# A gated block kernel on one Trainium2 core: values' hi and lo parts in one stationary operand, gate steps from output block 2, a lone step as one chunk

## The chip, the cores and the metric

The kernel runs on 1 core of one Trainium2 chip. The metric is the device time of one execution in microseconds (us). The kernel before takes 708.98 us, the median of 3 runs (708.42 to 709.07). The profile comes from one execution of 709.15 us, whose first and last instructions lie 707.1 us apart (the span).

## The reference

One residual block for 512 positions of 1024 features, one layer, batch 1, all in float32. Cut to what matters:

```python
proj = rms_norm(x, norm_mix_g) @ w_in
cb, cc, cin, q, k, v, f_logit, g_logit = split(proj)
y_conv = (cb * causal_dwconv(cc * cin, conv_mix_w)) @ w_out_conv
o = forgetting_attention(q, k, v, cumsum(log_sigmoid(f_logit + b_f)))   # 8 heads of 64
y_attn = o @ w_out_attn
g_conv, g_attn = split(sigmoid(g_logit + b_gate))                       # 1024 each
x = x + (g_conv * y_conv + g_attn * y_attn) @ w_o
a, b = split(causal_dwconv(rms_norm(x, norm_ffn_g) @ w_up, conv_ffn_w)) # 2816 each
x = x + (silu(a) * b) @ w_down
return rms_norm(x, norm_f_g)
```

## The kernel before, in words

**Products.** Everything is stored with features on the 128 partitions and the 512 positions along the free axis. Each float32 operand is kept as two parts, hi (its rounding to the matmul's input format) and lo (the rest). One product of a 128x128 weight block with activations is then three matmuls: hi weight with hi activation, lo weight with hi, hi weight with lo. `mm3` (L272, matmuls at L280) issues them for a whole block in two column halves of 256; `passes` (L286, matmuls at L298) does the same for a list of products.

**The stream of weights.** All weights come in chunks of up to 128x1024 in one fixed order, the list `stream` (L118 to L141). For a chunk, `load` (L157) starts the DMA on SyncE's queue into a raw tile (L170), several chunks ahead, and `split` (L230) makes the hi part on ScalarE (ACT, L249) and the lo part on VectorE (DVE, L253). These tiles are called raw_X, wh_X and wl_X after the chunk; wh and wl have two buffers each, so a split waits until TensorE is through with the chunk two ahead of it. Behind each split stands a budget in us by the chunk's kind, and `run_later` (L211) spends it: it takes work from the list `later`, whose items carry an assumed cost, and stops at the first one that is due and too dear. So `later` and those numbers fix where a small job stands in the in-order queues of ACT and DVE between two splits. `flush` issues what has to be done at once.

**Stages.** First the v projection, then those for q and k of two head pairs. Then the attention loop (L714 to L726): per unit (head pair, head, block of 128 queries) it issues the scores, half of another projection (`fill`) to keep TensorE busy, the transposes of the softmaxed scores of three units earlier (`transp`, tile tp; ACT writes their hi part pth, DVE at L605 their lo part ptl), and after each fourth unit `attend`. Scores use PSUM banks 3 and 4 in turn, transposes 5 and 6. During this loop DMA queues also make "forms", sums of weight blocks, in DRAM (`make_forms` L178: puts on SyncE's queue, accumulating DMAs on GpSimd's, one or two per loop slot).

`attend` (L607) forms, in bank 7 (tile o), the output of both heads of a pair for half of the queries. For each head e and block of keys it runs `mm3` with 128 columns of stationary weights, of which 64 are the head's values and 64 are zeros, so that both heads accumulate into the same 256 columns, each in its own 64 partitions. The values' hi and lo parts are two tiles, vh and vl. Then ACT copies o into oth (L621) and DVE subtracts into otl (L622).

**The merge stage** (L899 to L925) loops over eight output blocks j. For each it needs two gates: g(j) and g(8+j). For j = 0 to 2 they are plain projections (chunks in(20+j) and in(28+j), 48 matmuls each); the variable GJ = 3 says from which block on they come from `seven` (L743): a two-by-two block product in 7 instead of 8 products, with sums of weight blocks (the forms) and sums of activation blocks. Such a step of two products has a P chunk (18 matmuls) and an F chunk with the DMA-made forms (24 matmuls); an output block takes P, F, P, F. It writes four PSUM banks, (0, 1, 5, 6), where the products' sums are then combined (`gate_pair`). The activations' sums are made once from a fresh copy of x, xt: GpSimd's queue loads it (L809), ACT scales it by the norm's gain (L816, eight instructions), DVE forms sums (L824 to L829), ACT makes the hi part xth (L835) and DVE the lo part xtl (L836). This work is in `later` from chunk mix1 on. Then follows chunk mix(j), 48 matmuls into two banks, yc and ya; DVE multiplies them by the gates (L921, L922), GpSimd adds (L923), ACT and DVE split into mh and ml (L924, L925). The banks come from `acc`, a ring in the order 3, 4, 5, 6, 0, 1, 2, 7: mix0 has 3 and 4, in21 and in29 have 5 and 6, mix1 has 0 and 1, in22 and in30 have 2 and 7.

**The rest.** W_o, then the up projection and the gated unit in two phases, each followed by 7-product steps for W_down (20 steps of a P and an F chunk each; one step of phase 2 is a lone product, 9 + 12 matmuls), whose results `combine` adds to x1 (L1081 to L1099), also through `later`. For phase 2 it adds there `final_square` (L1107), per output block two ACT instructions and one DVE instruction into ssq, for the last norm. Two output blocks come from plain matmuls with the chunks dp0 to dp2 into banks 6 (pdA), 7 and 0 (pdB). The sums of squares go through pc_n and pb_n, and the output is scaled and written.

Of the kernel before, what the change touches and what calls it, by code (L numbers as in the profile page):

```python
# [50 lines left out]
)  # L51
HELD = 2

GJ = 3
GATES = tuple(((j, q), (j, q + 1)) for j in range(GJ, KB) for q in (0, 2))

PLAIN = [(m, k) for m in (6, 7) for k in range(*PHASES[1])]
# [7 lines left out]
def block_kernel(ctx, tc, xT, vecs, wv, win, wmix, wo, wup, wst, wdp, outT):  # L65
# [164 lines left out]
    def split(hl=None):  # L230

        k = len(parts)
        if k == len(stream):
            return
        nm, _, ncol = stream[k]
        load(k + (LOOK if len(raws) > KB else AHEAD))
        if hl is None:
            hl = []
            for x in "hl":
                if k == 0:  # L240
                    wp.tile([P, PADW[x]], F32, tag=f"pad{x}", name=f"pad_{x}")
                hl.append(wp.tile([P, D], F32R, tag=f"w{x}", name=f"w{x}_{nm}", bufs=2)[:, :ncol])
        hi, lo = hl
        raw = raws[k]
        if k == 0:
            for cs in (slice(0, VW), slice(VW, S + H)):
                keep(nc.vector.tensor_copy(hi[:, cs], raw[:, cs]))
        else:
            ins = nc.scalar.activation(hi, raw, AF.Copy)  # L249
            order["hi"] = ins.ins  # L250
            if k < KB:
                keep(ins)
        ins = nc.vector.tensor_sub(lo, raw, hi.bitcast(F32))  # L253
# [98 lines left out]
    def ct(name):  # L352
        return ap.tile([P, S], F32, tag="ct", name=name, bufs=NCT)
# [12 lines left out]
    )  # L366


    vh = ap.tile([P, NT, 4, 3, HD], F32R, tag="vh", name="vh")
    vl = ap.tile([P, NT, 4, 3, HD], F32R, tag="vl", name="vl")  # L370
    for t in (vh, vl):
        nc.gpsimd.memset(t.bitcast(F32)[:, :, :, 1, :], 0.0)
# [27 lines left out]
    def square_x(kb):  # L400
        if kb == 0:
            keep(nc.scalar.activation(ssq, xs[kb], AF.Square))
            return
        sq = ap.tile([P, S], F32, tag="pp", name=f"sq{kb}", bufs=NPP)
        keep(nc.scalar.activation(sq, xs[kb], AF.Square))
        keep(nc.vector.tensor_add(ssq, ssq, sq))

# [197 lines left out]
        nc.vector.tensor_sub(tl[:, : qb + 1, rs], src, th.bitcast(F32)[:, : qb + 1, rs])  # L605

    def attend(pr, half):  # L607
        o = bank(7, f"o{pr}{half}")
        nk = 2 * half + 2
        for e in range(2):  # L610
            th, tl = PT.pop((pr, e, half))
            for kb in range(nk):
                cs = slice(P, 2 * P) if kb == nk - 1 else slice(0, 2 * P)
                wh = vh[:, kb, pr, e : e + 2, :].rearrange("p a b -> p (a b)")
                wl = vl[:, kb, pr, e : e + 2, :].rearrange("p a b -> p (a b)")
                mm3(
                    o[:, cs], wh, wl, th[:, kb, cs], tl[:, kb, cs],
                    e == 0 and kb == 0, e == 1 and kb == nk - 1,
                )
        hs = slice(half * 2 * P, (half + 1) * 2 * P)  # L620
        nc.scalar.activation(oth[:, pr, hs], o[:, : 2 * P], AF.Copy)  # L621
        nc.vector.tensor_sub(otl[:, pr, hs], o[:, : 2 * P], oth.bitcast(F32)[:, pr, hs])  # L622


    def run_all(fs):
# [35 lines left out]
    def evac_v(g, t):  # L661
        p = (pa, pb)[g][t]
        src = p[:, : 4 * HD].rearrange("p (a b c) -> p a b c", a=2, b=2)
        pr = slice(2 * g, 2 * g + 2)
        for e in range(2):
            nc.scalar.activation(vh[:, t, pr, 2 * e, :], src[:, :, e, :], AF.Copy, scale=rc1[:, t : t + 1])
            nc.vector.scalar_tensor_tensor(
                vl[:, t, pr, 2 * e, :], src[:, :, e, :], rc1[:, t : t + 1],
                vh.bitcast(F32)[:, t, pr, 2 * e, :], op0=ALU.mult, op1=ALU.subtract,
            )  # L670


# [70 lines left out]
    def seven(doubles, n0, sets, operand, goes_on=None, stays=None, done=None):  # L743


        todo, wants = [], {}
        for n, d in enumerate(doubles):
            for kind in "PF":
                prods = []
                for s_, (i, q) in enumerate(d):  # L750
                    for f, g, b, h in PROD:
                        if (f < 3) == (kind == "P"):
                            wants.setdefault(f"{kind}{n0 + n}", []).append(("q", q))
                            c = 3 * s_ + f if f < 3 else s_ + len(d) * (f - 3)
                            prods.append((c, i, operand(q, g), b, h))
                todo.append((f"{kind}{n0 + n}", prods))
        users = [{(i, b) for _, i, _, b, _ in prods} for _, prods in todo]
        for n, (name, prods) in enumerate(todo):
            wh, wl = chunk(name)
            flush(wants[name])  # L760
            before = set().union(*users[:n])
            after = set().union(*users[n + 1 :])
            out = []
            for c, i, (xh, xl), b, h in prods:
                if i not in open_:
                    flush(sets[i])
# [7 lines left out]
            if name[0] == "F":  # L774
# [62 lines left out]

        return f

    k = [c[0] for c in stream].index("mix1")  # L840
    for q in (0, 2):
        f, g = x_sums(slice(q, q + 2))
        for i in (q, q + 1):
            later.append((k, 0, (("q", i),), x_scale(i)))
        later.append((k, 1.4, (("q", q),), f))
        later.append((k, 1.5, (("q", q),), g))
        for i in (q, q + 1):
            later.append((k + 1, 1.25, (("q", i),), x_split(i)))
        k += 2

    def gate_form(q, g):
        if g < 3:
# [219 lines left out]
    def combine(ph, i, banks, ids):  # L1072
# [248 lines left out]
```

## Time and profile before

| what | value |
|---|---|
| median of 3 runs | 708.98 us |
| the profiled execution | 709.15 us, span 707.1 us |
| TensorE (PE) busy | 99% of the span, 6054 matmuls |
| VectorE (DVE) busy | 70%, 766 instructions |
| ScalarE (ACT) busy | 48%, 525 instructions |
| GpSimd (POOL) busy | 25% |
| mean granted TensorE clock | 0.997 |

The profile gives times in us from the span's start; L12 is line 12 of the kernel. A group's row has its duration for one instruction in ns; the durations of matmuls overlap, so that their pitch has to be taken from starts. In a timeline the row begins with the start and the duration, and a bracket at its end gives the idle time of the engine before it and the instruction that ended it. The list of waits gives total, count and longest in us. A row of windows gives, for PE, weight loads, DVE, ACT and POOL, the busy us, then the granted clock, the DMA share and GB/s.

### The profile page before, as it was taken

The page shows a single profiled execution, that of the slowest core. Times are in us where ns is not written, and L with a number is a line of the kernel's source. Part 1 is how long each engine was busy: PE and PEld are TensorE (multiplying, and loading weights), DVE is VectorE, ACT ScalarE, POOL GpSimd, SP SyncE. Part 2 cuts the span into 40 slices and gives each one's busy share as a digit, 9 for nine tenths or more (in the row PEclk, how much of TensorE's full clock was granted, in tenths as well). Part 3 has the DMA queues.
Part 4 walks back from the last instruction along what each step waited for, and adds up shares of the span by engine and source line. Part 5 has one row for each costly group of instructions (what it writes and reads, how often), then busy time and mean ns, then how long its engine had stood idle before and what let it go on. Part 6 is the DMA issues. An engine that isn't in the chain of part 4 may idle for free. (4 is left out here: it accounts for less than half of the span.)

```text
span 707.1 us, 14653 instructions
## 1 busy us (share of the span) xinstructions
PE 696.6 (99%) x6054; PEld 694.6 (98%) x6054; DVE 494.6 (70%) x766; ACT 336.7 (48%) x525; POOL 174.0 (25%) x189
## 2 busy tenths in 40 slices
PE   9999999999999999999999999999999999999995
PEld 9999999999999999999999999999999999999995
DVE  6677767665477877854468777777774677877783
ACT  6664545453455544444354444445443345544562
POOL 5124847432101000134513223010000322311002
PEclk9999999999999999999999999999999999999998
DMA  7427979532451455687976856554636686676403
GB/s 249 165 73 246 198 201 205 111 89 68 129 208 53 149 183 175 198 281 188 222 177 170 211 118 147 141 178 159 203 128 227 142 194 154 179 188 165 145 26 119
DMA packets 52690, 116.02 MB, mean 164 GB/s; under 512 B 4976, under 2 KB 23408, under 8 KB 52624
## 3 DMA queue, kind: packets, MB, share of 16 engines
q1 hardware_dynamic: 37456, 94.16, 41.2%
q0 software_dynamic: 13760, 19.70, 17.5%
q10 hardware_dynamic: 1408, 1.24, 0.5%
q8 instruction: 47, 0.77, 0.5%
q14 instruction: 19, 0.16, 0.1%
HBM read 112.92 MB, written 33.03 MB: 206 GB/s over the span
## 5 line engine op out<-in xcount | busy, mean ns | idle before, releaser
L280 PE MATMUL p_up<-x1l,wh_up 128*128 128x256 f32 x536 | 104.5, 276 | 0.0
L280 PE MATMUL p_up<-x1h,wh_up 128*128 128x256 f32 x536 | 104.4, 276 | 0.0
L280 PE MATMUL p_up<-x1h,wl_up 128*128 128x256 f32 x536 | 104.3, 276 | 0.0
L249 ACT ACTIVATE wh_up<-raw_up 128x1024 fp32r<-128x1024 f32 x44 | 46.7, 1060 | 89.1 <-PE p_up L280 68.8
L280 PEld LDWEIGHTS p_up<-x1l,wh_up 128*128 128x128 f32 x536 | 80.8, 188 | 0.0
L280 PEld LDWEIGHTS p_up<-x1h,wh_up 128*128 128x128 f32 x536 | 80.7, 188 | 0.0
L280 PEld LDWEIGHTS p_up<-x1h,wl_up 128*128 128x128 f32 x536 | 80.6, 188 | 0.0
L253 DVE TENSOR_TENSOR wl_up<-raw_up,wh_up 128x1024 fp32r<-128x1024 f32 x44 | 53.8, 1223 | 20.6 <-ACT wh_up L249 20.6
L280 PE MATMUL p_in<-xgh,wh_in 128*128 128x256 f32 x288 | 56.9, 279 | 1.1 <-ACT wh_in L249 1.1
L1034 POOL TENSOR_TENSOR ge<-fu,fu 128x512 f32<-128x512 f32 x11 | 17.1, 1551 | 161.6 <-DVE fu L530 150.9
L280 PE MATMUL p_in<-xgl,wh_in 128*128 128x256 f32 x288 | 56.5, 277 | 0.0
L280 PE MATMUL p_in<-xgh,wl_in 128*128 128x256 f32 x288 | 56.4, 277 | 0.0
L198 POOL DMA_DIRECT2D f<-in_wst_dram x48 | 56.4, 1293 | 0.0
L1021 DVE TENSOR_TENSOR fz<-p_up,rb_n 128x512 f32<-128x512 f32 x44 | 30.3, 690 | 31.5 <-PE p_up L280 31.5
L253 DVE TENSOR_TENSOR wl_F<-raw_F,wh_F 128x1024 fp32r<-128x1024 f32 (+1 forms) x30 | 40.4, 1346 | 14.3 <-ACT wh_F L249 14.3
L280 PEld LDWEIGHTS p_in<-xgh,wh_in 128*128 128x128 f32 x288 | 44.7, 188 | 1.9 <-ACT wh_in L249 1.2
L249 ACT ACTIVATE wh_F<-raw_F 128x1024 fp32r<-128x1024 f32 (+1 forms) x30 | 31.6, 1052 | 30.3 <-PE dn L298 25.9
L280 PEld LDWEIGHTS p_in<-xgl,wh_in 128*128 128x128 f32 x288 | 43.6, 188 | 0.0
L280 PEld LDWEIGHTS p_in<-xgh,wl_in 128*128 128x128 f32 x288 | 43.5, 188 | 0.0
L298 PE MATMUL p_up<-x1h,wh_up 128*128 128x256 f32 x168 | 40.3, 277 | 0.0
L298 PE MATMUL p_up<-x1l,wh_up 128*128 128x256 f32 x168 | 40.2, 276 | 0.0
L253 DVE TENSOR_TENSOR wl_in<-raw_in,wh_in 128x1024 fp32r<-128x1024 f32 x26 | 34.7, 1336 | 7.3 <-ACT wh_in L249 6.8
(306 smaller groups left out, 2050.5 us busy)
## 6 DMA issues: line engine op xcount, KB each, us to landing
raw_up<-in_wup_dram SPq DMA_DIRECT2D x44, 512.0 KB, 4.7
raw_F<-f SPq DMA_DIRECT2D x29, 512.0 KB, 4.3
raw_in<-in_win_dram SPq DMA_DIRECT2D x26, 512.0 KB, 3.5
raw_P<-in_wst_dram SPq DMA_DIRECT2D x29, 384.0 KB, 3.9
f<-in_wst_dram POOLq DMA_DIRECT2D x29, 256.0 KB, 5.7
f<-in_wst_dram SPq DMA_DIRECT2D x14, 512.0 KB, 6.0
f<-in_wst_dram POOLq DMA_DIRECT2D x14, 512.0 KB, 8.1
f<-f SPq DMA_DIRECT2D x28, 256.0 KB, 4.6
```

The lines of the kernel that those rows point to most:

```text
L198: return lambda: keep(nc.gpsimd.dma_start(dst, src, accum_op=ALU.add))
L249: ins = nc.scalar.activation(hi, raw, AF.Copy)
L253: ins = nc.vector.tensor_sub(lo, raw, hi.bitcast(F32))
L280: keep(nc.tensor.matmul(out[:, cs], w, x[:, cs], start=start and i == 0 and c == 0, stop=stop and i == 2 and c == len(cut) - 1,))
L298: keep(nc.tensor.matmul(out, wl if x == 1 else wh, xl if x == 2 else xh, start=opens and bk not in seen, stop=closes and bk not in left,))
L1021: nc.vector.tensor_mul(z, p, rb2)
L1034: keep(nc.gpsimd.tensor_mul(ge, a.rearrange(halves_of, h=2), b.rearrange(halves_of, h=2)))
```

## The change

1. **Values.** vh and vl become one tile v2 that holds, for each head, the 64 columns of hi and the 64 of lo side by side. One matmul then gives hi and lo products at once, so that each head and block of keys takes two matmuls (with pth and with ptl) instead of three; it also adds the product of the two lo parts. The two heads go to separate halves of bank 7. The hi and lo products lie in different partitions, and so per head ACT copies one of them (L630) and DVE adds the other (L631) into a tile oc, before oth (L633) and otl (L634) are made from oc. The two memsets of the zero columns go.
2. **Gates.** GJ is 2: output block 2 takes P0, F0, P1, F1 (84 matmuls) instead of in22 and in30 (96). There are 12 gate steps instead of 10, and 6 groups of forms to be made by DMA instead of 5. The work on xt moves: it is due from chunk in29 on, with other assumed costs.
3. **Buffers.** One square tile of the first stage is allocated earlier, and the pool of xt waits for the last reader of each tile whose space it takes over.
4. **The lone step** is one chunk S (two DMAs, one split, 21 matmuls) instead of P and F.
5. **final_square** has the assumed cost 1.5 instead of 0.8 in `later`.

The core of the diff:

```diff
-GJ = 3
+GJ = 2
...
     def step_chunks(n):
         m = len(DOUBLES[n])
+        if m == 1:
+            return [(f"S{n}", n, NF * P)]
...
+            elif nm[0] == "S":
+                keep(nc.sync.dma_start(raw[:, : 3 * P], wst[src, :, : 3 * P]))
+                keep(nc.sync.dma_start(raw[:, 3 * P : ncol], made[src]))
...
-        run_later(k, {"u": 1.7, "P": 1.6, "F": 0.75, "i": 3.0, "m": 3.0}.get(nm[0], 3.5))
+        run_later(k, {"u": 1.7, "P": 1.6, "F": 0.75, "S": 1.6, "i": 3.0, "m": 3.0}.get(nm[0], 3.5))
...
+    v2 = ap.tile([P, NT, 4, 2, 2, HD], F32R, tag="v2", name="v2")
 
     ssq = ct("ssq1")
+    sq1 = ap.tile([P, S], F32, tag="pp", name="sq1", bufs=NPP)
...
     def attend(pr, half):
         o = bank(7, f"o{pr}{half}")
         nk = 2 * half + 2
         for e in range(2):
-            th, tl = PT.pop((pr, e, half))
+            parts_ = PT.pop((pr, e, half))
             for kb in range(nk):
-                cs = slice(P, 2 * P) if kb == nk - 1 else slice(0, 2 * P)
-                wh = vh[:, kb, pr, e : e + 2, :].rearrange("p a b -> p (a b)")
-                wl = vl[:, kb, pr, e : e + 2, :].rearrange("p a b -> p (a b)")
-                mm3(
-                    o[:, cs], wh, wl, th[:, kb, cs], tl[:, kb, cs],
-                    e == 0 and kb == 0, e == 1 and kb == nk - 1,
-                )
+                c0 = P if kb == nk - 1 else 0
+                w = v2[:, kb, pr, e, :, :].rearrange("p a b -> p (a b)")
+                for i, x in enumerate(parts_):
+                    keep(nc.tensor.matmul(
+                        o[:, 2 * P * e + c0 : 2 * P * (e + 1)], w, x[:, kb, c0:],
+                        start=e == 0 and kb == 0 and i == 0, stop=e == 1 and kb == nk - 1 and i == 1,
+                    ))
+        oc = ap.tile([P, 2 * P], F32, tag="oc", name=f"oc{pr}{half}")
+        for e in range(2):
+            own, other = slice(e * HD, (e + 1) * HD), slice((1 - e) * HD, (2 - e) * HD)
+            cs = slice(2 * P * e, 2 * P * (e + 1))
+            nc.scalar.activation(oc[own], o[other, cs], AF.Copy)
+            nc.vector.tensor_add(oc[own], o[own, cs], oc[own])
         hs = slice(half * 2 * P, (half + 1) * 2 * P)
-        nc.scalar.activation(oth[:, pr, hs], o[:, : 2 * P], AF.Copy)
-        nc.vector.tensor_sub(otl[:, pr, hs], o[:, : 2 * P], oth.bitcast(F32)[:, pr, hs])
+        nc.scalar.activation(oth[:, pr, hs], oc, AF.Copy)
+        nc.vector.tensor_sub(otl[:, pr, hs], oc, oth.bitcast(F32)[:, pr, hs])
...
-    xp = ctx.enter_context(tc.tile_pool(name="xp", bufs=1, side="right"))
+    xp = ctx.enter_context(tc.tile_pool(name="xp", bufs=1, side="right", reuse_waits="tile"))
...
-    k = [c[0] for c in stream].index("mix1")
-    for q in (0, 2):
-        f, g = x_sums(slice(q, q + 2))
+    k = [c[0] for c in stream].index(f"in{28 + GJ - 1}")
+    for q in range(4):
+        later.append((k, 0, (("q", q),), x_scale(q)))
+    for q, d, us in ((0, (0, 1), (1.4, 0.6)), (2, (1, 2), (0.9, 0.8))):
+        for f in x_sums(slice(q, q + 2)):
+            later.append((k + d[0], us[0], (("q", q),), f))
         for i in (q, q + 1):
-            later.append((k, 0, (("q", i),), x_scale(i)))
-        later.append((k, 1.4, (("q", q),), f))
-        later.append((k, 1.5, (("q", q),), g))
-        for i in (q, q + 1):
-            later.append((k + 1, 1.25, (("q", i),), x_split(i)))
-        k += 2
+            later.append((k + d[1], us[1], (("q", i),), x_split(i)))
...
-                later.append((0, 0.8, (), lambda m=m: final_square(m)))
+                later.append((0, 1.5, (), lambda m=m: final_square(m)))
```

The lines shift by 4 to 12: DVE's products L921 and L922 are L931 and L932 in the changed kernel, xt's sums L836 to L841, xtl L848.

**Where it moves instructions.** The first place is VectorE in the attention loop, around the attend of pair 2, second half (s and m are a unit's scores and row sums). Before:

```order
L577 ISA s312_2262,m312_2265<-s312_2262,strip_101 128x384
L577 ISA m312_2265 128x1
L622 TENSOR_TENSOR otl_95<-o21_2235,oth_94 128x256
L584 RECIPROCAL m312_2265<-m312_2265 128x1
L577 ISA s303_2313,m303_2316<-s303_2313,strip_101 128x512
```

In the changed kernel:

```order
L581 ISA s312_2260,m312_2263<-s312_2260,strip_101 128x384
L581 ISA m312_2263 128x1
L631 TENSOR_TENSOR oc21_2253<-o21_2236,oc21_2253 64x256
L588 RECIPROCAL m312_2263<-m312_2263 128x1
L631 TENSOR_TENSOR oc21_2253<-o21_2236,oc21_2253 64x256
L634 TENSOR_TENSOR otl_95<-oc21_2253,oth_94 128x256
L581 ISA s303_2311,m303_2314<-s303_2311,strip_101 128x512
L581 ISA m303_2314 128x1
```

Three instructions on oc and otl stand where one stood, each waiting for ACT's one ahead of it in the chain, and only a reciprocal stands between them.

The second place is the start of output block 2 in the merge stage. TensorE in the changed kernel, from the end of mix1 (ya1) into P0, with the rows that wait for another engine marked (dn025, dn020 and dn021 are the banks 5, 0 and 1):

```order
L285 MATMUL ya1_2802<-oth_94,wl_mix1_2725 128x256 x2
L285 MATMUL ya1_2802<-otl_95,wh_mix1_2724 128x256 x2
L303 MATMUL dn025_2858<-xgh_92,wh_P0_2790 128x256 [waits DVE_49,Activation_49]
L303 MATMUL dn025_2858<-xgl_93,wh_P0_2790 128x256
L303 MATMUL dn020_2856<-xgh_92,wh_P0_2790 128x256 [waits DVE_49]
L303 MATMUL dn020_2856<-xgl_93,wh_P0_2790 128x256
L303 MATMUL dn021_2857<-xth_2579,wh_P0_2790 128x256 [waits DVE_49]
L303 MATMUL dn021_2857<-xtl_2580,wh_P0_2790 128x256
```

Before, in22 stood there, with only its own weights to wait for:

```order
L280 MATMUL ya1_2792<-oth_94,wl_mix1_2713 128x256 x2
L280 MATMUL ya1_2792<-otl_95,wh_mix1_2712 128x256 x2
L280 MATMUL p_ga2_2846<-xgh_92,wh_in22_2780 128x256 [waits Activation_49]
L280 MATMUL p_ga2_2846<-xgh_92,wh_in22_2780 128x256
L280 MATMUL p_ga2_2846<-xgh_92,wl_in22_2781 128x256 [waits DVE_49]
L280 MATMUL p_ga2_2846<-xgh_92,wl_in22_2781 128x256
```

VectorE at the same place before (g1 and g9 are block 1's gates):

```order
L829 SCALAR_TENSOR_TENSOR xt_2582<-xt_2582 128x2x256
L253 TENSOR_TENSOR wl_in22_2781<-raw_in22_2545,wh_in22_2780 128x1024
L836 TENSOR_TENSOR xtl_2584<-xt_2582,xth_2583 128x1024 x2
L800 TENSOR_TENSOR g9_2788<-p_gb1_2727,rb_n1_530 128x512
L921 TENSOR_TENSOR g1_2724<-g1_2724,yc1_2791 128x512
L922 TENSOR_TENSOR g9_2788<-g9_2788,ya1_2792 128x512
L253 TENSOR_TENSOR wl_in30_2900<-raw_in30_2704,wh_in30_2899 128x1024
L925 TENSOR_TENSOR ml_2589<-g1_2724,mh_2588 128x512
```

and in the changed kernel:

```order
L258 TENSOR_TENSOR wl_P0_2791<-raw_P0_2544,wh_P0_2790 128x768
L840 SCALAR_TENSOR_TENSOR xt_2578<-xt_2578 128x2x256
L812 TENSOR_TENSOR g9_2798<-p_gb1_2739,rb_n1_527 128x512
L841 SCALAR_TENSOR_TENSOR xt_2578<-xt_2578 128x2x256
L931 TENSOR_TENSOR g1_2736<-g1_2736,yc1_2801 128x512
L848 TENSOR_TENSOR xtl_2580<-xt_2578,xth_2579 128x1024 x2
L932 TENSOR_TENSOR g9_2798<-g9_2798,ya1_2802 128x512
L258 TENSOR_TENSOR wl_F0_2879<-raw_F0_2700,wh_F0_2878 128x1024
L935 TENSOR_TENSOR ml_2585<-g1_2736,mh_2584 128x512
```

The product of g9 with ya1 came directly behind that of g1 with yc1, and has now two instructions on xtl ahead of it, as xt's work moved up to this place.

The third place is VectorE in the tail, around the split of dp0 (x1 is the residual, cz10 and cu10 belong to the combine of i = 0, cz11 to that of i = 1). Before:

```order
L1081 TENSOR_TENSOR cz10_8507<-dn2200_8264,cz10_8507 128x256
L253 TENSOR_TENSOR wl_P29_8535<-raw_P29_8344,wh_P29_8534 128x768
L1084 TENSOR_TENSOR x1_3968<-dn2206_8262,x1_3968 128x512
L1088 TENSOR_TENSOR cu10_8539<-dn2201_8265,cz10_8507 128x256
L1089 TENSOR_TENSOR x1_3968<-dn2207_8263,x1_3968 128x256
L253 TENSOR_TENSOR wl_F29_8561<-raw_F29_8374,wh_F29_8560 128x1024
L1092 TENSOR_TENSOR x1_3968<-x1_3968,dn2207_8263 128x512
L253 TENSOR_TENSOR wl_dp0_8590<-raw_dp0_8402,wh_dp0_8589 128x1024
L1095 TENSOR_TENSOR x1_3968<-x1_3968,cz10_8507 128x512
L1099 TENSOR_TENSOR x1_3968<-x1_3968,cu10_8539 128x512
L1084 TENSOR_TENSOR x1_3968<-dn2212_8441,x1_3968 128x512
L1115 TENSOR_TENSOR ssq3_4492<-ssq3_4492,sq3_0_8595 128x512
```

and in the changed kernel:

```order
L258 TENSOR_TENSOR wl_F31_8551<-raw_F31_8351,wh_F31_8550 128x1024
L258 TENSOR_TENSOR wl_dp0_8579<-raw_dp0_8407,wh_dp0_8578 128x1024
L1125 TENSOR_TENSOR ssq3_4498<-ssq3_4498,sq3_5_8582 128x512
L1091 TENSOR_TENSOR cz10_8586<-dn2400_8269,cz10_8586 128x256
L1094 TENSOR_TENSOR x1_3974<-dn2406_8267,x1_3974 128x512
L1098 TENSOR_TENSOR cu10_8590<-dn2401_8270,cz10_8586 128x256
L1099 TENSOR_TENSOR x1_3974<-dn2407_8268,x1_3974 128x256
L1102 TENSOR_TENSOR x1_3974<-x1_3974,dn2407_8268 128x512
L1105 TENSOR_TENSOR x1_3974<-x1_3974,cz10_8586 128x512
L1109 TENSOR_TENSOR x1_3974<-x1_3974,cu10_8590 128x512
L258 TENSOR_TENSOR wl_dp2_8600<-raw_dp2_8496,wh_dp2_8599 128x1024
L1125 TENSOR_TENSOR ssq3_4498<-ssq3_4498,sq3_0_8603 128x512
```

The combine of i = 0 (cz10 to its last x1) and a sum of squares moved from ahead of the split of dp0 to behind it.

More of the change, by code (lines that the diff above doesn't have):

```diff
@@ L366, in block_kernel @@
     )
[L369 to L372, printed above, removed]
+    v2 = ap.tile([P, NT, 4, 2, 2, HD], F32R, tag="v2", name="v2")
     ssq = ct("ssq1")
+    sq1 = ap.tile([P, S], F32, tag="pp", name="sq1", bufs=NPP)
     pa = [bank(t, f"pa{t}") for t in range(NT)]
@@ L403, in square_x @@
             return
-        sq = ap.tile([P, S], F32, tag="pp", name=f"sq{kb}", bufs=NPP)
+        sq = sq1 if kb == 1 else ap.tile([P, S], F32, tag="pp", name=f"sq{kb}", bufs=NPP)
         keep(nc.scalar.activation(sq, xs[kb], AF.Square))
@@ L665, in evac_v @@
         for e in range(2):
-            nc.scalar.activation(vh[:, t, pr, 2 * e, :], src[:, :, e, :], AF.Copy, scale=rc1[:, t : t + 1])
+            nc.scalar.activation(v2[:, t, pr, e, e, :], src[:, :, e, :], AF.Copy, scale=rc1[:, t : t + 1])
             nc.vector.scalar_tensor_tensor(
-                vl[:, t, pr, 2 * e, :], src[:, :, e, :], rc1[:, t : t + 1],
-                vh.bitcast(F32)[:, t, pr, 2 * e, :], op0=ALU.mult, op1=ALU.subtract,
+                v2[:, t, pr, e, 1 - e, :], src[:, :, e, :], rc1[:, t : t + 1],
+                v2.bitcast(F32)[:, t, pr, e, e, :], op0=ALU.mult, op1=ALU.subtract,
             )
@@ L747, in seven @@
         for n, d in enumerate(doubles):
-            for kind in "PF":
+            for kind in "PF" if len(d) > 1 else "S":
                 prods = []
@@ L751, in seven @@
                     for f, g, b, h in PROD:
-                        if (f < 3) == (kind == "P"):
+                        if kind == "S" or (f < 3) == (kind == "P"):
                             wants.setdefault(f"{kind}{n0 + n}", []).append(("q", q))
-                            c = 3 * s_ + f if f < 3 else s_ + len(d) * (f - 3)
+                            c = f if kind == "S" else 3 * s_ + f if f < 3 else s_ + len(d) * (f - 3)
                             prods.append((c, i, operand(q, g), b, h))
@@ L773, in seven @@
             passes(out, len(out))
-            if name[0] == "F":
+            if name[0] in "FS":
                 for i in sorted({i for _, i, *_ in prods}):
```

## The prediction

> **What bounds the kernel now.** I read the page's busy times and clock first, then TensorE's list of waits, then the timelines of the three places that the change touches.
>
> ```profile
> PE 696.6 (99%) x6054; PEld 694.6 (98%) x6054; DVE 494.6 (70%) x766; ACT 336.7 (48%) x525; POOL 174.0 (25%) x189
> ...
> PEclk9999999999999999999999999999999999999998
> ```
>
> TensorE is busy 696.6 of 707.1 us, at the full granted clock. What it waits for is short enough to list whole:
>
> ```profile
> PE p_in L280 <- ACT wh_in L249: 1.1, 1, 1.1
> PE warm L108 <- DVE ones L100: 1.0, 1, 1.0
> PE dn L298 <- ACT wh_F L249: 0.8, 1, 0.8
> PE pdA L280 <- DVE wl_dp L253: 0.3, 1, 0.3
> PE pc_n L313 <- ACT sq L1183: 0.3, 1, 0.3
> PE pb_n L327 <- POOL rc_n L320: 0.2, 1, 0.2
> ```
>
> They sum to 3.7 us. So a removed matmul is worth its full pitch, and other engines count only where they open a new hold of TensorE. There are two questions: how many matmuls go, and which holds appear.
>
> **The matmul's pitch.** The profile's 276 ns is a latency of overlapping matmuls. The pitch comes from starts:
>
> ```profile
> 97.55 0.37 PE L280 MATMUL o<-pth,vh 128*128 128x256 f32 x1
> ...
> 98.67 0.22 PE L280 MATMUL o<-pth,vh 128*128 128x128 f32 x1
> ...
> 98.95 0.33 PE L280 MATMUL o<-pth,vh 128*128 128x256 f32 x1
> ...
> 100.32 0.39 PE L572 MATMUL s<-a_k,a_q 128*128 128x384 f32 x1
> ```
> ```profile
> 188.89 0.45 PE L280 MATMUL yc<-ych,wh_mix 128*128 128x256 f32 x2
> ...
> 194.40 0.39 PE L280 MATMUL p_ga<-xgh,wh_in 128*128 128x256 f32 x2
> ```
> ```profile
> 205.28 0.39 PE L280 MATMUL yc<-ych,wh_mix 128*128 128x256 f32 x2
> ```
>
> The 96 matmuls of in21 and in29 lie between 194.40 and 205.28: 10.88/96 = 0.1133 us each. The second mix, 48 of them, takes 5.44. In attention the three 128-column matmuls from 98.67 to 98.95 take 0.28, 0.093 each.
>
> **Term 1, attention.** This view lists the tile o:
>
> ```profile
> L280 PE MATMUL o<-pth,vl x48: 273/276/283, 83.2 to 188.7; 128*128 128x256 f32 x32, 128*128 128x128 f32 x16
> ...
> L621 ACT ACTIVATE oth<-o x8: 378/384/385, 84.6 to 189.1; 128x256 fp32r<-128x256 f32 x8
> L622 DVE TENSOR_TENSOR otl<-o,oth x8: 415/420/422, 85.4 to 189.7; 128x256 fp32r<-128x256 f32 x8
> ```
>
> One such group of 48 goes (three products become two): 32 x 0.1133 + 16 x 0.093 = 5.1 us less. With 0.06 or 0.11 for a short one the bounds are 4.6 and 5.4. I take **-5.1**.
>
> In exchange each attend gets two ACT copies and two DVE adds, 16 of each, by the rows above 0.38 and 0.42 us and in a chain. They must stay hidden beside TensorE. DVE is fullest here:
>
> ```profile
> 120.00:130.00 10.00, 10.00 (x89) 10.00 (x88) 8.65 (x18) 6.28 (x15) 4.24 (x6) 1.00 0.56 146
> ```
> ```profile
> 125.27 0.27 PE L601 MATMUL tp<-ident,pp 128*128 128x128 f32 x1
> ```
> ```profile
> 121.49 0.68 DVE L605 TENSOR_TENSOR ptl<-tp,pth 128x512 fp32r<-128x512 f32 x1
> ```
>
> A transpose needs a PSUM bank that the ptl two units earlier has emptied: the one at 125.27 needs the ptl that ended at 122.17, 3.1 us of cover. In the changed order DVE waits inside the chain: from the first add to otl 3 x 0.42 + 2 x 0.38 = 2.03 us instead of 0.42, so later ptl come up to 1.6 late. That is under 3.1, so I cost it at 0; the other end is rival A. The sixth group of forms adds three POOL and three SP DMA issues; with POOL at 4.24 of 10 and the weights loaded far ahead I cost these at 0 too. The two memsets that go stand beside busy TensorE: 0.
>
> **Term 2, gate steps.** Block 2 takes 2 x (18 + 24) = 84 matmuls in steps instead of 96 in two projections: 12 x 0.1133 = **-1.4**.
>
> **Term 3, the hold at the first gate step.** Before, in22 stood behind mix1 and wrote banks 2 and 7. Now P0 does, and it writes banks 5, 0, 1; banks 0 and 1 are those of mix1's yc and ya. Its third matmul waits for DVE's g1*yc1 and its fifth for g9*ya1, which stands behind two xtl in DVE's queue (order rows above). The durations, all of before:
>
> ```profile
> 195.69 2.13 DVE L253 TENSOR_TENSOR wl_in<-raw_in,wh_in 128x1024 fp32r<-128x1024 f32 x1 [0.34 <-ACT wh_in L249]
> ...
> 203.02 0.69 DVE L824 TENSOR_TENSOR xt<-xt 128x512 f32<-128x512 f32 x1
> ...
> 206.63 1.23 DVE L253 TENSOR_TENSOR wl_in<-raw_in,wh_in 128x1024 fp32r<-128x1024 f32 x1 [0.67 <-ACT wh_in L249]
> 207.77 2.36 DVE L836 TENSOR_TENSOR xtl<-xt,xth 128x1024 fp32r<-128x1024 f32 x2
> 210.04 0.69 DVE L800 TENSOR_TENSOR g<-p_gb,rb_n 128x512 f32<-128x512 f32 x1
> 210.64 0.68 DVE L921 TENSOR_TENSOR g<-g,yc 128x512 f32<-128x512 f32 x1
> ```
> ```profile
> 194.60 1.06 ACT L249 ACTIVATE wh_in<-raw_in 128x1024 fp32r<-128x1024 f32 x1 [2.12 <-PE ya L280]
> 196.77 0.64 ACT L924 ACTIVATE mh<-g 128x512 fp32r<-128x512 f32 x1 [1.11 <-POOL g L923]
> ...
> 201.05 2.55 ACT L816 ACTIVATE xt<-xt,vec 128x512 f32<-128x512 f32 x4
> ...
> 206.50 1.99 ACT L835 ACTIVATE xth<-xt 128x1024 fp32r<-128x1024 f32 x2
> ```
>
> By starts a DVE instruction of 512 columns takes 0.60 in a row (210.04 to 210.64), a wl 1.14, the pair of xtl 2.27; on ACT an x scaling 0.62, an xth 1.0. Time 0 is mix0's start (188.89 before). wh_in29 starts at +5.7 before; now the sigmoids behind attend's longer chain end at +6.2, so it ends at +7.2. ACT then has all eight scalings (4.96), mh (0.55) and wh_mix1 (1.06): +13.8. DVE, which did wl_in29, four xt and ml meanwhile, goes on: wl_mix1 1.14, two xtl 2.27, then seven instructions (two xt, g1, xt's third and fourth, wl_P0 of 768 columns at 0.87, midway between 0.60 and 1.14, and g9), 6 x 0.60 + 0.87 = 4.5: +21.7. g1*yc1 ends at +22.3. The next xtl waits for its xth on ACT (1.05 after +21.7) and ends, with its twin, at +25.0; g9*ya1 ends at +25.75. TensorE: mix0, in21 with in29, mix1 are 5.44 + 10.88 + 5.44, so P0 starts at +21.76, its third matmul is due at +22.0 and held 0.3, its fifth is due at +22.5 and held 3.2. I take **+3.5**. Even directly behind ya's end (+22.0) the product would hold 0.5, the lower bound; were everything on DVE as slow as wl_in at 195.69 (2.13 for 1.23) it would be 5. F0's weights are due only at +27.9 and no second hold follows. xt itself is there: in before POOL issues it at 189.66 after this wait, now behind the last scores.
>
> ```profile
> 189.66 2.24 POOL L809 DMA_DIRECT2D xt<-in_xT_dram  x4 [12.87 <-PE o L280]
> ```
>
> **Term 4, the tail.** S29 has the 21 matmuls of P27 and F27. DVE's queue is the matter:
>
> ```profile
> 667.58 0.28 PE L298 MATMUL dn<-gh,wh_P 128*128 128x256 f32 x1
> ...
> 673.37 0.39 PE L298 MATMUL dn<-gh,wh_F 128*128 128x256 f32 x1 [0.83 <-ACT wh_F L249]
> ```
> ```profile
> 690.25 0.47 PE L313 MATMUL pc_n<-ones,ssq 128*128 128x1 f32 x3
> ```
> ```profile
> 679.01 1.23 DVE L253 TENSOR_TENSOR wl_dp<-raw_dp,wh_dp 128x1024 fp32r<-128x1024 f32 x1 [0.24 <-ACT wh_dp L249]
> ...
> 684.19 0.42 DVE L1081 TENSOR_TENSOR cz<-dn,cz 128x256 f32<-128x256 f32 x1
> 684.53 1.22 DVE L253 TENSOR_TENSOR wl_dp<-raw_dp,wh_dp 128x1024 fp32r<-128x1024 f32 x1
> ```
> ```profile
> 680.00:690.00 10.00, 9.71 (x85) 9.51 (x84) 9.64 (x18) 6.83 (x13) 0.00 (x0) 1.00 0.01 2
> ```
>
> From the lone step to pc_n it takes 690.25 - 667.58 = 22.67 now. The squares that ACT had ahead of wh_F go behind it: the 0.83 hold goes, and wl_dp0 comes at 11.43 - 0.83 = +10.6. But one ssq and five pieces of the combine of i=0, before ahead of wl_dp0, now stand behind it. From wl_dp0 to the last ssq DVE has 2 wl, 13 of 512 columns and 9 of 256 (0.34 by 684.19 to 684.53): 2 x 1.14 + 13 x 0.60 + 9 x 0.34 = 13.1, without a gap, since it was 9.64 of 10 busy already. pc_n at +23.8: **+1.1**. Bounds: -1.1 (both holds, 0.83 and 0.29, go and nothing is late) and +1.7 (ACT's last square adds a gap).
>
> **Sum.** -5.1 - 1.4 + 3.5 + 1.1 = -1.9 against the profiled execution's 709.15 (span 707.1 and 2.05 around it): 707.25. That execution lies 0.17 above the median of 708.98, so the forecast is **707.1**.
>
> **Rivals.**
> A, slower: attend's chain uncovers the transposes. Place: DVE between an attend and the next two ptl, where a 1.23 wl or 1.7 of other work follows. If half of the 1.6 us comes through at each of the eight, 6.4: **713.5**. From 0.24 per attend (1.9/8) the gain is gone. For it: 8.65 of 10 busy; against: 3.1 of cover.
> B: no long hold at P0, because DVE runs ahead or xtl is taken elsewhere: 0.5 instead of 3.5, **704.1**. Against it: DVE is in order, and xtl stands ahead.
> C: the hold lowers the clock.
>
> ```profile
> 700.00:708.00 8.00, 0.33 (x3) 0.14 (x2) 1.95 (x4) 0.39 (x1) 1.27 (x1) 0.66 0.38 131
> ```
>
> TensorE ended at 700.33, and a mean of 0.66 over 8 us, if the clock is 1 and then 0.5, means a fall at 702.6, 2.2 us later. A 3.2 us hold is longer. If matmuls then ran at half speed for as long as the hold, it costs 1.6 more: **708.7**. Against it: holds of 1.06 and 0.83 left the clock at 1.00. [...]
> D: the merged stationary operand gains nothing (128 columns of weights are loaded at each matmul and weight loads are 694.6 busy): only terms 2 to 4 are left, +3.2: **712.2**. Against it: pitch followed the count of matmuls in both places above.
>
> **How the numbers follow.** About 0.2% (1.4 us) is what a measurement can tell from no change. The forecast has 0.50, between 704.4 and 709.6 by its bounds: 0.32 of that faster, 0.18 same. A 0.14 (slower), B 0.18 (faster), C 0.12 (same), D 0.06 (slower). So faster 0.50, same 0.30, slower 0.20. The range takes in the forecast's, B and C and a mild A: 703.5 to 710.4.
>
> **What would show it.** Term 1: tile o with 96 matmuls, a second-half attend of 1.85 instead of 2.77, no tp among TensorE's waits (else A). Term 3: in the waits a dn held by DVE, 3 to 3.5 in all, with P0; near 0.5 means B, granted clock below 1 just behind it C. Term 4: no wh_F hold, pc_n held about 2 by ssq. If the time is over 710.4 without tp in the waits, D or a hold that I missed made the prediction wrong.

## The result, and the profile after

The changed kernel takes 709.93 us, the median of 12 runs (708.63 to 711.65), the kernel before 708.74 us (708.42 to 709.12, 12 runs): a ratio of 1.0013, with an interval of 1.0004 to 1.0022. It is a little slower, where 707.1 was forecast. The spread is part of the result: 3.0 us instead of 0.7. The runs lie on levels, and a level goes with the mean granted clock of the run:

| runs of the changed kernel | us | mean clock |
|---|---|---|
| 5 | 708.63 to 708.91 | 0.995 |
| 6 | 709.93 to 710.42 | 0.990 to 0.993 |
| 1 | 711.65 | 0.988 |

The kernel before has no such levels: its 41 runs beside the experiments lie between 708.3 and 709.3, with 0.995 to 0.998. The profiled execution took 708.69 us (span 706.5), so it is one of the lowest level. Even there the clock was not full throughout, as its windows below show.

First the page's busy times, then the top of TensorE's list of waits (total, times, longest, in us):

```profile
PE 691.2 (98%) x5994; PEld 689.1 (98%) x5994; DVE 503.5 (71%) x788; ACT 344.3 (49%) x543; POOL 175.1 (25%) x190
```
```profile
PE dn L303 <- DVE g L932: 3.0, 1, 3.0
PE pc_n L318 <- DVE ssq L1199: 2.1, 1, 2.1
PE p_in L285 <- ACT wh_in L254: 1.1, 1, 1.1
PE warm L108 <- DVE ones L100: 1.0, 1, 1.0
PE pdA L285 <- DVE x L1094: 0.6, 1, 0.6
...
```

The 60 matmuls that were to go are gone, and both holds stand where the prediction put them: P0 for g9*ya1, and pc_n for the last sum of squares. wh_F's hold of 0.8 is gone. No transpose waits.

TensorE's timeline at the places where the stages begin gives each term. The start of the first attend (the kernel before first, then the changed one), the second half of an attend, mix0, P0 with its hold, the lone step and pc_n:

```profile
82.98 0.37 PE L280 MATMUL o<-pth,vh 128*128 128x256 f32 x1
```
```profile
82.84 0.37 PE L622 MATMUL o<-pth,v 128*128 128x256 f32 x1
```
```profile
96.91 0.37 PE L622 MATMUL o<-pth,v 128*128 128x256 f32 x1
...
98.78 0.39 PE L576 MATMUL s<-a_k,a_q 128*128 128x384 f32 x1
```
```profile
183.32 0.45 PE L285 MATMUL yc<-ych,wh_mix 128*128 128x256 f32 x2
```
```profile
205.15 0.28 PE L303 MATMUL dn<-xgh,wh_P 128*128 128x256 f32 x1
...
205.82 0.28 PE L303 MATMUL dn<-xgl,wh_P 128*128 128x256 f32 x1
209.14 0.38 PE L303 MATMUL dn<-xth,wh_P 128*128 128x256 f32 x1 [3.04 <-DVE g L932]
...
210.90 0.28 PE L303 MATMUL dn<-xgh,wh_F 128*128 128x256 f32 x1
```
```profile
664.36 0.28 PE L303 MATMUL dn<-gh,wh_S 128*128 128x256 f32 x1
...
687.90 0.58 PE L318 MATMUL pc_n<-ones,ssq 128*128 128x1 f32 x4 [2.07 <-DVE ssq L1199]
```

An attend's second half takes 1.87 instead of 2.77 us, and mix0 starts 188.89 - 183.32 = 5.57 earlier. Of that, 0.14 lies ahead of the first attend; from there to mix0 it is 105.91 before and 100.48 now, 5.43 less. From P0 to F0 it is 5.75, where 18 matmuls take 2.04: 3.7 of hold and slower pitch around it. From the lone step to pc_n it is 23.54 instead of 22.67. At pc_n the changed kernel is 690.25 - 687.90 = 2.35 us ahead. At the end it is ahead by 0.6. The other 1.7 are lost behind pc_n, where no instruction changed. Windows of 3.41 us (the length for which the clock stays down in this trace; columns PE, weight loads, DVE, ACT, POOL, granted clock) show it:

```profile
682.12:685.54 3.42, 3.42 (x32) 3.42 (x32) 3.42 (x8) 1.01 (x2) 0.00 (x0) 1.00 0.00 0
685.54:688.95 3.41, 1.34 (x12) 1.18 (x11) 1.85 (x4) 2.86 (x7) 0.00 (x0) 0.99 0.00 0
688.95:692.36 3.41, 3.41 (x17) 3.41 (x18) 0.23 (x2) 0.00 (x0) 0.71 (x1) 0.51 0.02 5
```

Behind the hold of 2.1 the granted clock is 0.5 for 3.41 us, so half of that, 1.7 us, is lost; the count of matmuls in the window falls from 32 to 17.

### The profile page after: what moved, and what is told of

It is laid out like the page before. It is cut to its first block, busy times and chain, and to the rows that moved or that the text cites. A ratio compares the mean times of both kernels' runs of the same rounds, so it can differ in the third digit from the quotient of the medians.

```text
span 706.5 us, 14597 instructions
## 1 busy us (share of the span) xinstructions
PE 691.2 (98%) x5994; PEld 689.1 (98%) x5994; DVE 503.5 (71%) x788; ACT 344.3 (49%) x543; POOL 175.1 (25%) x190
## 4 chain that ended last, share of the span: by engine, by line
PE 92%; DVE 3%; ACT 3%; issue 1%; POOL 0%; DVEq 0%; ACTq 0%
PE p_up L285 26%; PE dn L303 21%; PE p_in L285 14%; PE p_up L303 8%; PE p_wo L285 6%; PE ya L285 2%; PE yc L285 2%; PE pa L439 2%; PE pb L441 2%; PE p_q L285 2%; PE p_k L285 2%; PE o L622 1%; PE tp L605 1%; PE pdB L285 1%; PE s L576 1%; PE s L577 1%
## 5 line engine op out<-in xcount | busy, mean ns | idle before, releaser
L203 POOL DMA_DIRECT2D f<-in_wst_dram x51 | 58.5, 1277 | 0.0
L258 DVE TENSOR_TENSOR wl_F<-raw_F,wh_F 128x1024 fp32r<-128x1024 f32 x31 | 42.1, 1359 | 14.4 <-ACT wh_F L254 14.4
L254 ACT ACTIVATE wh_F<-raw_F 128x1024 fp32r<-128x1024 f32 x31 | 33.0, 1066 | 26.9 <-PE dn L303 23.0
L254 ACT ACTIVATE wh_P<-raw_P 128x768 fp32r<-128x768 f32 x31 | 26.2, 844 | 29.6 <-PE dn L303 23.4
```

What stands on the lines that cost most here:

```text
L203: return lambda: keep(nc.gpsimd.dma_start(dst, src, accum_op=ALU.add))
```

## The experiments

Two theories stood against each other. Theory 1: the sum of the prediction holds at full clock, and each of the two holds also halves the clock for a while, which falls differently from run to run. The rival: holds cost their length and no more, and what is missing is a smaller gain elsewhere. All ratios are to the kernel before, run beside them.

**e1: part 1 alone.** The kernel before with the diff's v2, its filling and attend, nothing else.

> The kernel before with part 1 alone (values' hi and lo in one stationary operand). Theory 1 (the gain of attention is there in full, and what is lost is lost in two holds and in the clock behind them): mix0 starts 5.4 to 5.6 us earlier than before's 188.89, no tp in the list of waits, no hold over 1.1, granted clock as before (0.997) and a spread as narrow as before's 0.7: about 5.5 below the kernel before, 703.3. Rival (attend's longer chain holds the transposes, or merged operands gain less): less than 4 below it.

703.31 us (702.92 to 703.46, 4 runs), ratio 0.9921 (0.9908 to 0.9934). The profile's mix0 starts at 183.15, 5.74 earlier, of which 5.4 lies between the first attend and mix0 as in the whole change. The waits are those of the kernel before; its longest are:

```profile
PE warm L108 <- DVE ones L100: 1.0, 1, 1.0
PE p_in L280 <- ACT wh_in L249: 1.0, 1, 1.0
PE dn L298 <- ACT wh_F L249: 0.9, 1, 0.9
PE pdA L280 <- DVE wl_dp L253: 0.3, 1, 0.3
...
```

So attention's gain is there in full, and rival A (the transposes) is out. All that the whole change loses against this kernel, 6.6 us, comes from its other parts.

**e2 and e3: one hold taken away at a time.** In e2 mix1 has banks 2 and 7:

```diff
-    acc = ring(3, 4, 5, 6, 0, 1, 2, 7)
+    acc = ring(3, 4, 5, 6, 2, 7, 0, 1)
-                acc = ring(2, 7, 3, 4)
+                acc = ring(3, 4, 2, 7)
```

> The changed kernel with mix1 in banks 2 and 7 instead of 0 and 1, so that P0 waits for none of mix1's products. Theory 1: the hold of 3.3 at P0 goes; the tail's hold of 2.1 stays and halves the clock for one window of 3.4 us in some runs: two levels, 703.7 without and 705.4 with the drop, mean clock 0.997 and 0.995. Rival (the clock costs nothing, holds count by their length alone): one level, 709.9 - 3.3 = 706.6.

In e3 final_square has its old cost:

```diff
-                later.append((0, 1.5, (), lambda m=m: final_square(m)))
+                later.append((0, 0.8, (), lambda m=m: final_square(m)))
```

> The changed kernel with final_square's assumed cost back at 0.8. Theory 1: the tail's hold at pc_n goes (0.9 by the stage's length) and with it the clock's drop behind it (1.7); the hold at P0 stays and drops the clock in some runs: two levels, about 706.1 without and 707.8 with it. Rival (no cost by the clock): one level, 709.9 - 0.9 = 709.0.

| kernel | runs | us | mean clock |
|---|---|---|---|
| e2 (tail's hold left) | 4 | 704.82 to 705.29 | 0.997 |
| | 5 | 706.17 to 707.06 | 0.993 to 0.995 |
| | 3 | 708.11 to 708.43 | 0.991 |
| e3 (P0's hold left) | 1 | 705.40 | 0.997 |
| | 4 | 706.88 to 707.18 | 0.993 to 0.995 |

The levels are there in both, their means 1.4 to 1.9 apart, and the clock tells them apart; each hold drops it by itself. The medians are 706.24 (ratio 0.9965, 0.9954 to 0.9975) and 706.99 (0.9970, 0.9958 to 0.9982). The one-level rival is out. e3's two levels lie 0.7 to 0.8 below what was expected. e2 has a third level, and its undropped one lies 1.3 above what was expected. The list of waits says why: with P0's hold gone, F0 waits for wh_F, and block 2 from P0 to mix2 takes 10.94 instead of 84 x 0.1133 = 9.52.

```profile
PE pc_n L318 <- DVE ssq L1199: 2.1, 1, 2.1
...
PE dn L303 <- ACT wh_F L254: 0.7, 1, 0.7
PE pdA L285 <- DVE x L1094: 0.6, 1, 0.6
```

**e4: both edits.**

> The changed kernel with both edits: other banks for mix1 and final_square at 0.8. Theory 1: no hold over 1.1 is left, so the clock does not drop before the end: one level, 702.8 (708.7 - 1.7 - 3.3 - 0.9), spread under 1, mean clock 0.997. Rival (the clock costs nothing): 709.9 - 3.3 - 0.9 = 705.7; if another hold appears instead, its time is added.

703.27 us (702.85 to 703.52, 5 runs), ratio 0.9920 (0.9907 to 0.9933), mean clock 0.996 to 0.997: one level, as narrow as that of the kernel before, though 0.5 above the 702.8 expected. It is no better than part 1 alone (703.31), although block 2 has 12 matmuls less. In the profile P0 starts at 205.14, F0 at 208.04 and P1 at 211.32: 2.90 and 3.28 instead of 2.04 and 2.72. The hold moved to F0, whose wh stands behind two xth in ACT's queue:

```profile
208.04 0.38 PE L303 MATMUL dn<-xgh,wh_F 128*128 128x256 f32 x1 [0.70 <-ACT wh_F L254]
```
```profile
205.03 2.02 ACT L847 ACTIVATE xth<-xt 128x1024 fp32r<-128x1024 f32 x2
206.95 1.04 ACT L254 ACTIVATE wh_F<-raw_F 128x1024 fp32r<-128x1024 f32 x1
```

**e5 and e6: x's third and fourth split one chunk later**, with e4's banks and with those of the change:

```diff
-            later.append((k + d[1], us[1], (("q", i),), x_split(i)))
+            later.append((k + d[1] + (i >= 2), us[1], (("q", i),), x_split(i)))
```

> The kernel of e4 with x's third and fourth split (xth, xtl) one chunk later, behind F0's weights. In e4 the gate steps of block 2 won nothing: F0 waited 0.86 for wh_F and about 0.6 more up to P1, behind two xth and two xtl. Theory 1: these waits go: 703.3 - 1.5 = 701.8, one level. Rival (F0's weights are late by their DMA or by wh's buffer): 703.3 again.

> The changed kernel with final_square at 0.8 and x's third and fourth split one chunk later, banks as in the change. Theory 1: g9*ya1 stands directly behind g1*yc1, the hold at P0 is 0.5 to 0.7 and drops no clock: one level, 702.4. Rival (the bank itself, not the two xtl, makes the hold): 3 us of hold stay, 705.4 to 707.0 as in e3.

e5: 702.98 us (702.72 to 703.30, 5 runs), ratio 0.9918 (0.9904 to 0.9931). e6: 703.22 (702.99 to 703.41, 4 runs), 0.9920 (0.9906 to 0.9933). e6 shows that the two xtl made the hold at P0, not the banks by themselves: with them behind g9*ya1 the hold is gone while the banks are those of the change. But neither e6's 702.4 nor e5's 701.8 came. In e5 F0 starts on time, 2.04 behind P0, and P1 now takes 3.41 instead of 2.04, since it waits for the xtl that was moved:

```profile
210.66 0.28 PE L303 MATMUL dn<-xth,wh_P 128*128 128x256 f32 x1
212.01 0.39 PE L303 MATMUL dn<-xtl,wh_P 128*128 128x256 f32 x1 [1.07 <-DVE xtl L848]
```

**e7 and e8: the hold at P0 made shorter and longer**, both with final_square at 0.8. Theories 1a and 1b are two guesses of the author at how much of a window has to be idle, for these runs to decide between. In e7 only x's fourth split comes later (`(i == 3)` in the line above); in e8 the second xtl is computed three times over, with the same values:

```diff
-            nc.vector.tensor_sub(xql[:, q], xq[:, q], xqh.bitcast(F32)[:, q])
+            for _ in range(3 if q == 1 else 1):
+                nc.vector.tensor_sub(xql[:, q], xq[:, q], xqh.bitcast(F32)[:, q])
```

> The kernel of e3 with only x's fourth split one chunk later: one xtl less ahead of g9*ya1, a hold of 2.1 to 2.2 at P0. Without a drop of the clock 705.4 - 1.1 = 704.3. Theory 1a (a window of 3.4 us halves the next one if about two thirds of it or more are idle; 2.2 us are at most 64%): seldom or never a drop, 704.3 in all runs. Theory 1b (half of a window is enough): a drop in most runs, 705.9. [...]

> The kernel of e3 with the second xtl computed three times (the same values), 2.3 us more of VectorE ahead of mix1's products: a hold of about 5.5 at P0. Theories 1a and 1b: the clock drops in every run, for one window of 3.4 us or two: 705.4 + 2.3 + 1.6 = 709.3, or 711. [...] Rival (no cost by the clock): 707.7 in all.

e7: 706.22 us (5 runs): one of 704.38 and four of 706.19 to 706.53, ratio 0.9958 (0.9946 to 0.9971); its hold was 1.9. e8: 708.64 (708.01 to 709.81, 11 runs), ratio 0.9998 (0.9989 to 1.0006), mean clock 0.991 to 0.995 in every run; its hold was 4.4, not 5.5, so that by e3's 705.40 with 3.0 of hold it would stand at 706.8 at full clock, and every run lies 1.2 to 3.0 above that. So the clock costs something in every run of e8, as theories 1a and 1b had it. Theory 1a fell by e7: a hold of 1.9 was enough in four of five runs. The windows of the profiled executions say how much idling it takes. The three of e7 around P0, then two of the changed kernel at its P0 (no drop follows), then three of e8:

```profile
205.94:209.36 3.42, 1.46 (x10) 1.18 (x10) 2.83 (x4) 2.52 (x3) 0.86 (x1) 1.00 0.00 0
209.36:212.77 3.41, 3.41 (x18) 3.41 (x17) 3.41 (x4) 1.36 (x2) 1.33 (x1) 0.50 0.52 173
212.77:216.19 3.42, 3.42 (x32) 3.42 (x31) 1.70 (x2) 1.17 (x2) 0.00 (x0) 1.00 0.26 103
```
```profile
204.25:207.67 3.42, 1.79 (x14) 1.39 (x12) 2.83 (x5) 3.29 (x4) 0.00 (x0) 1.00 0.00 0
207.67:211.08 3.41, 1.94 (x16) 1.94 (x17) 2.55 (x3) 0.32 (x1) 1.91 (x1) 1.00 0.02 5
```
```profile
204.52:207.93 3.41, 1.51 (x12) 1.15 (x10) 3.41 (x6) 2.49 (x3) 0.00 (x0) 1.00 0.00 0
207.93:211.35 3.42, 0.95 (x3) 0.86 (x4) 3.42 (x5) 1.74 (x3) 0.33 (x1) 0.50 0.00 0
211.35:214.76 3.41, 3.41 (x17) 3.41 (x17) 1.54 (x3) 1.37 (x2) 1.86 (x1) 0.50 0.47 123
```

Of these windows, those with TensorE busy for 1.34 (the tail), 1.46 or 1.51 of 3.41 us were followed by half clock, those with 1.79 or 1.94 were not. That fits theory 1b. Behind e8's second window, busy for 0.95, the clock was at 0.50 in the third too. In the changed kernel's profiled execution, by an estimate from its fall at 688.89 (141 steps of 3.413 us back), a window's edge near 207.6 cut the long hold at P0 into two halves, and nothing followed: 1.00 up to 211.08.

But half of a window busy is not the rule, as the ends of the same kernels show. In e6 a window there is busy for 2.22 us and half clock follows; many of its matmuls are only one column wide (pc_n):

```profile
691.17:694.59 3.42, 2.22 (x15) 1.75 (x14) 0.38 (x2) 1.19 (x3) 0.87 (x2) 1.00 0.27 95
694.59:698.00 3.41, 0.00 (x0) 0.00 (x0) 1.73 (x4) 0.00 (x0) 1.10 (x1) 0.50 0.63 219
```
```profile
691.52 0.61 PE L318 MATMUL pc_n<-ones,sq 128*128 128x1 f32 x4 [0.27 <-ACT sq L1193]
691.99 0.96 PE L1216 MATMUL warm_to<-gl,gh 128*128 128x256 f32 x6
693.15 0.71 PE L332 MATMUL pb_n<-ident,rc_n 128*128 128x128 f32 x4 [0.20 <-POOL rc_n L325]
```

In e2 the 3.41 us ahead of a fall at 699.6 at the end (0.90 over the second row is 0.4 us at half clock) were busy for about 2.56:

```profile
696.00:698.00 2.00, 1.73 (x16) 1.64 (x15) 0.55 (x2) 0.92 (x2) 0.22 (x1) 1.00 0.54 190
698.00:700.00 2.00, 1.03 (x7) 0.64 (x5) 0.25 (x1) 0.38 (x1) 0.68 (x2) 0.90 0.00 0
700.00:706.00 6.00, 0.00 (x0) 0.00 (x0) 1.70 (x4) 0.00 (x0) 1.06 (x1) 0.50 0.50 175
```

What sorts the windows better is how many columns the matmuls begun in them move, counted in the timelines of the same profiles:

| clock in the window | columns, and where the window starts | clock in the next |
|---|---|---|
| 1.00 | 520 (changed kernel, 685.5), 2052 (e6, 691.17), 2304 (e7, 205.94, and e8, 204.52), 2560 (e2, 682.55) | 0.50 |
| 1.00 | 3072, 4096 and 3336 (changed kernel, 204.2, 207.6 and 695.7) | 1.00 |
| 0.50 | 768 (e8, 207.93), 2056 (e2, 685.96) | 0.50 |
| 0.50 | 3584 (e2, 689.38), 3840 (changed kernel, 688.9), 4096 (e7, 209.36) | 1.00 |

At the pitch of 0.1133, 30 matmuls of 256 columns, 7680, fit in a window. In the two profiles of the kernel before and the changed one, counted in steps of 3.413 us from their falls, no window at full clock with fewer than 3072, from 8 us on, was followed by full clock. One end does not fit, by an estimate: e5's last 2300 or so columns begin at 690.4 and are through at 693.60, but its mean clock of 0.998 over 700.5 us leaves about 2.8 us of half clock, a fall near 697.7, where e6 has it at 694.59 behind the like.

In two profiles the edges of the clock lie whole windows apart: in the changed kernel it falls at 688.89, rises at 692.30 and falls at 702.54, which is 1 and then 3 times 3.413 us; in e2 it falls at 685.96, rises at 692.79 and falls at 699.6, which is 2 and then 2 times. That the windows run on like this through an execution, that a hold falls on them differently from run to run and that the levels come from this is the author's estimate; no run shows an edge moved on purpose.

**e9: GpSimd scales xt**, behind its load, and x's third split goes back ahead of F0:

```diff
-                nc.scalar.activation(xt[:, kb, :], xt[:, kb, :], AF.Copy, scale=col(G1 + kb))
+                nc.gpsimd.tensor_scalar(
+                    xt[:, kb, :], xt[:, kb, :], col(G1 + kb), 0.0, op0=ALU.mult, op1=ALU.add
+                )
...
-        later.append((k, 0, (("q", q),), x_scale(q)))
+        x_scale(q)()
```

> The kernel of e5 with xt's scaling on GpSimd (eight instructions right behind its load) instead of ScalarE, and x's third split back ahead of F0's weights. In e5 the hold of block 2's first step only moved on, to P1's wait of 1.4 for xtl. Theory 1 (the work on xt is what limits the start of block 2, and ACT's eight scalings are its first 5 us): the chain comes some 1.4 us sooner and P1 waits no more: 703.0 - 1.4 = 701.6. Rival (wh_F0, which waits for the end of mix1 on TensorE, and not xt, sets when xtl can come; or GpSimd beside VectorE slows both): 703 or more.

703.15 us (702.55 to 703.26, 5 runs), ratio 0.9919 (0.9906 to 0.9933): nothing won, and theory 1 of this run fell. GpSimd had scaled xt by 183, but VectorE's first sum still ran only at 192.74, in its place in the queue. From wl_mix at 195.58 to the end of block 2's second wl_P VectorE has a single gap, of 0.55, and P1 waits for this wl_P:

```profile
211.02 0.94 DVE L258 TENSOR_TENSOR wl_P<-raw_P,wh_P 128x768 fp32r<-128x768 f32 x1
```
```profile
212.01 0.51 PE L303 MATMUL dn<-xgh,wl_P 128*128 128x256 f32 x2 [0.87 <-DVE wl_P L258]
```

So in e4, e5 and e9 three different instructions held block 2, for 1.5, 1.4 and 1.2 us in all. That points to VectorE's load in these 16 us, which none of the three lowers, as the cause behind them; sums ahead of mix0's products, where VectorE still has gaps, weren't tried.

In these 16 us an instruction of VectorE takes longer while GpSimd's addition of mix1's products runs. First e5's rows, then e9's:

```profile
206.11 2.10 DVE L258 TENSOR_TENSOR wl_F<-raw_F,wh_F 128x1024 fp32r<-128x1024 f32 x1 [0.35 <-ACT wh_F L254]
```
```profile
205.84 1.30 POOL L933 TENSOR_TENSOR g<-g,g 128x512 f32<-128x512 f32 x1 [14.44 <-DVE g L932]
```
```profile
208.17 2.32 DVE L850 TENSOR_TENSOR xtl<-xt,xth 128x1024 fp32r<-128x1024 f32 x1
```
```profile
207.20 2.21 POOL L935 TENSOR_TENSOR g<-g,g 128x512 f32<-128x512 f32 x1 [15.47 <-DVE g L934]
```

VectorE's instruction takes 2.1 to 2.3 there and 1.2 where nothing runs on GpSimd (1.21 for e5's xtl at 210.75 and e9's wl_F at 211.89). In e9 the wl_F under which the addition begins, at 207.03, takes 1.22, and the addition 2.21 instead of e5's 1.30. The 0.9 to 1.1 us more are about what P1 waits for in these two kernels. That the addition makes the wait is not shown: no run moves it away.

**e10: part 4 undone in e5**, that is, without the chunk S.

> The kernel of e5 with part 4 undone: the lone step is a P and an F chunk again. Theory 1 (part 4 matters only where ACT and DVE hold the tail): wh_F's hold of 0.8 comes back and pdA's of 1.2 goes to 0.3 as in the kernel before, between 702.9 and 703.6. Rival (the chunk S itself is a gain): 703.7 or more.

703.85 us (703.38 to 704.14, 5 runs), ratio 0.9928 (0.9916 to 0.9941). It is 0.9 above e5, with wh_F's hold of 0.9 back and pdA's of 1.2 down to 0.3. By the time alone the rival (703.7 or more) took it. The profiled executions lie 1.2 apart: 0.56 of that lies between the first down step of phase 1 and pc_n (212.18 against 211.62), and another 0.7 ahead of mix0 (183.63 against 182.94), where the two kernels do the same. So the chunk S is worth some 0.6 here, the most that theory 1 gave it, and theory 1's claim that it matters only where ACT and DVE hold the tail stays unproven.

## Why the prediction was wrong

Its sum was right for an execution at full clock, as far as that can be worked out; no run of the changed kernel had full clock throughout. The profiled execution fell short of it by one drop of 1.7: 708.69 - 1.7 = 707.0, and 707.1 was forecast.

- **Term 1**, -5.1: measured -5.4 from the first attend to mix0, in the whole change and in e1. That is 48 x 0.1133. The prediction took the mean of three 128-column matmuls, 0.093. But of the three, the one with vl, which is the one that goes, takes 0.11 (rows of the kernel before):

```profile
98.73 0.28 PE L280 MATMUL o<-pth,vl 128*128 128x128 f32 x1
98.84 0.27 PE L280 MATMUL o<-ptl,vh 128*128 128x128 f32 x1
```

  The cost at nothing of the longer chain held.
- **Term 2**, -1.4, and **term 3**, +3.5: together +2.1, measured 2.35 from P0 to mix2 (13.23 against 10.88). The cause of the hold was as worked out, by e6. What the prediction did not see is that term 2 is not there to be had: once the hold goes, the same work on xt holds F0 or P1, for 1.2 to 1.5 us.
- **Term 4**, +1.1: measured +0.9; pc_n held 2.1 by ssq, pdA 0.6 by the combine.
- **The step that failed** is the cost of a lowered clock, which the sum puts at nothing. The prediction has it only as rival C, "the hold lowers the clock", with 0.12, at P0 alone and once. The runs show it at either hold: with one hold left, in 8 of 12 runs of e2 and in 4 of 5 of e3. The tail's hold of 2.1, for which no price of the clock was worked out at all, does it too, and is the one that did it in the profiled execution. One drop costs about 1.7, where C had 1.6; the median run, 2.9 above 707.0, has nearly two windows' worth. The row behind C was there: a fall of the clock 2.2 us after TensorE's end. The argument against it, holds of 1.06 and 0.83 without a fall, says nothing of holds of 1.9 and more.

The prediction's bounds for its forecast also add up to 704.6 and 709.7 rather than 704.4 and 709.6, which changes nothing.

In two profiles the clock stays down for a second window: e8's from 207.93 to 214.76, by the rows above, and e2's, with 6.8 us at 0.5, though TensorE was busy through the first half of it; but eight of the 16 matmuls begun there are pc_n's of one column:

```profile
685.96:689.38 3.42, 3.40 (x16) 3.42 (x17) 0.16 (x1) 0.52 (x2) 0.71 (x1) 0.50 0.00 0
689.38:692.79 3.41, 3.41 (x18) 3.41 (x18) 0.68 (x2) 0.67 (x2) 0.21 (x1) 0.50 0.02 5
```
```profile
685.98 0.98 PE L318 MATMUL pc_n<-ones,ssq 128*128 128x1 f32 x4 [2.10 <-DVE ssq L1199]
```

What stays open: what exactly the clock counts (the columns fit the windows counted here, but not e5's end), how many windows each unprofiled run lost, and what part 3, the earlier load of xt, is worth alone.

## What to carry to other kernels

Where TensorE is 98% busy, price a hold of about 2 us or more by its length plus, as a rival with a good chance, 1.7 us for a window of 3.4 us at half rate behind it. Here holds of 1.9 to 4.4 us dropped the clock in most runs (8 of 12 of e2, 4 of 5 of e3 and of e7, all 11 of e8), and kernels with no hold over 1.2 us (e1, e4, e5, e6, e9 and e10) had one level each, with a mean clock of 0.995 to 0.998; between the two nothing was measured. A spread that grows with a change, on levels that the mean clock tells apart, points to such a hold. And before matmuls are traded for VectorE work, add up VectorE's queue over that stage: here it had hardly a gap, and each cured wait came back at a later instruction.

## What was not expected of the hardware

- Between matmuls the clock's drop lasted 3.41 us (the changed kernel, e3, e7) or twice that (e2, e8). It followed windows in which few columns went through TensorE (520 to 2560, of some 7700), in e6 one in which TensorE was busy for 2.22 of 3.41 us.
- Executions of the changed kernel differed by steps of about 1.5 us: 708.7, 710.2 and 711.65.
- VectorE's instructions of 1024 columns took up to 2.32 (e9's xtl at 208.17) instead of 1.2 us while an addition ran on GpSimd.

The best median of these runs is e5's, 702.98 us, 0.8% below the kernel before. e1, with part 1 alone, is 0.3 us behind it, and their intervals overlap, so parts 2 to 5 are not shown to win anything.
